# RMS norms of a decoder layer: sums and 1/sqrt on a quarter of the tokens in each of four groups of 32 columns

## The chip, the cores and the metric

One program runs on one core of one Trainium2 chip. The metric is the device time of an execution in microseconds, as the median of several runs. The core has five engines with a queue each: TensorE (PE) for matmuls, VectorE (DVE) and ScalarE (ACT) for element-wise work, GpSimd (POOL), and SyncE (SP), which here only issues transfers. PE and PEld are TensorE's matmuls and its loads of weights.

## The reference, cut to what matters

```python
def _rmsnorm(x, g):
    ...
    y = xf * lax.rsqrt(jnp.mean(xf * xf, axis=-1, keepdims=True) + EPS)
...
    h = _rmsnorm(x, norm_mix_g)
    ...
    o_dn = _rmsnorm(o_dn, dn_norm_g) * jax.nn.silu(dn_z.astype(f32).reshape(B, L, DN_HEADS, DN_DV))
    ...
    h = _rmsnorm(x, norm_ffn_g)
...
    y_prompt = _rmsnorm(xp, norm_final_g)
    y_sample = _rmsnorm(xs, norm_final_g)
```

One layer with D_MODEL 2048 runs on 576 tokens (512 of a prompt and 8 times 8 new ones). A first norm precedes the mixer, which has eight gated delta-net heads and four mLSTM heads. Each delta-net head norms its output over its 128 features (`o_dn`). After the output projection comes the second norm, then a convolutional feed-forward network (FFN), then the last norm.

## The kernel before, in words

Activations lie transposed: features on the 128 partitions, tokens along the columns. A norm therefore needs a sum over partitions. `sum_bc` (L250) makes it on PE with a 128x128 matrix of ones: its result holds each token's sum of squares on all 128 partitions, so that what follows can be multiplied onto the activations directly. It takes two matmuls of 288 tokens in plain fp32 (L256). `rsqrt_bc` (L241) then makes 1/sqrt with a table function on ACT (L244) and one Newton step in four DVE operations (L245 to L248), all 128 partitions wide and 288 or 576 columns long.

The weight matmuls are split in three of a rounded format (`three`, L194, its matmul is L198): high times high, high times low, low times high, each on two halves of 288 tokens. Six of them make a step, after which `tick` runs. A tick advances the jobs: generators, in which `yield n` means "go on n ticks later". What a job issues on PE thus falls between two groups of six L198, and PE's order is fixed by the program. The order on DVE, ACT, POOL and SP is set by a scheduler at compile time. The weights come as `raw` through SP, and ACT (L120) and DVE (L121) split them into `wh` and `wl`.

The stages, in us of the profiled execution: start until 49, the mixer's input projection with the heads as jobs beside it until about 930, the output projection from about 950 to 1152, the FFN's up projection until 2165, the down projection until 2684 with the last 16 feature blocks in `down_last`, and the last norm.

**A delta-net head** (`dn_head`, L585) is a job. It starts when its inputs are projected, every 64 ticks, and when the head before the last one has ended. It begins with transposes and small products (L608 to L663), solves for the samples through memory (L809 to L834: `ud`, `xd`, `cx` are transfers), inverts blocks of 32, 64 and 128 (`inverse`, L778, which waits for the transposes L836 and starts on PE with L843), and goes through chunks with a state S (L676 to L696). At its end it norms its output: squares on ACT, six ticks later `sum_bc`, the chain of L244 to L248, the product with `rs_o` (L710), the gate, and a transfer of the head's output.

**The second norm** is `rms_bc2` (L1075), called in `ffn` (L1118) after the matmuls of the first FFN product. The sum of squares `acc[0]` comes from L1072.

**The last norm** is in `down_last` and `final` (L1524 and what follows it). The 16 blocks of features run first on tokens 0 to 319, then on tokens 320 to 575. A block (group) is 12 matmuls L1509, the eviction L1512 on DVE, the square L1514 on ACT, in the second pass also a scaling (L1522), and on every other block an addition (L1517). Each pass spawns a job `final`: three matmuls (L1534) add up three partial sums, then ACT L1536 and DVE L1537 to L1540. The job of the first pass runs two ticks into the second pass, a tick being one group there. The second pass's job ends the program: L1551 multiplies the scaled outputs, and they are written.

Of the kernel before, what the change touches and what calls it, by code (L numbers as in the profile page):

```python
# [8 lines left out]
F32 = mybir.dt.float32  # L9
F32R = mybir.dt.float32r  # L10
AF = mybir.ActivationFunctionType
ALU = mybir.AluOpType

P = 128
D = 2048
# [53 lines left out]
class Layer:  # L69
# [180 lines left out]
    def sum_bc(self, ss):  # L250

        pss = []
        for hf in range(2):
            pr = self.psr()
            sl = slice(hf * HALF, (hf + 1) * HALF)
            self.nc.tensor.matmul(pr[:, 0:HALF], self.ones, ss[:, sl], start=True, stop=True)  # L256
            pss.append((pr[:, 0:HALF], sl))
        return pss

    def rms_bc(self, ss, out):  # L260
        self.rsqrt_bc(self.sum_bc(ss), 1.0 / D, self.eps6, EPS, out, self.r(), self.r())
# [323 lines left out]
    def dn_head(self, h, q, k, v, sz):  # L585
# [116 lines left out]


        ob, sq2 = qe, q[:, 0:NT]
        sq, rs_o, a, u = kd, vs, KQ, X
        A.activation(sq, ob, AF.Square, scale=float(P) ** -0.5)
        Pl.tensor_tensor(out=sq, in0=sq, in1=sq2, op=ALU.add)
        yield 6
        self.rsqrt_bc(self.sum_bc(sq), 1.0, self.epsh, EPS * EPS * P, rs_o, a, u)
        V.scalar_tensor_tensor(out=ob, in0=ob, scalar=self.par[:, DG:DG + 1], in1=rs_o, op0=ALU.mult, op1=ALU.mult)  # L710
        Pl.tensor_tensor(out=ob, in0=ob, in1=sz, op=ALU.mult)
        self.later(12, self.mixd[h], ob)
# [359 lines left out]
            nc.vector.tensor_tensor(out=acc[0], in0=acc[0], in1=acc[1], op=ALU.add)  # L1072


    def rms_bc2(self, ss, out):  # L1075
        nc = self.nc
        V = nc.vector
        a = self.r()
        u = self.acc[1]
        for ps, sl in self.sum_bc(ss):  # L1080
            nc.scalar.activation(out[:, sl], ps, AF.Abs_reciprocal_sqrt, bias=self.eps6, scale=1.0 / D)
            V.tensor_scalar(out=a[:, sl], in0=ps, scalar1=1.0 / D, scalar2=EPS, op0=ALU.mult, op1=ALU.add)
        V.scalar_tensor_tensor(out=u, in0=out, scalar=-0.5, in1=out, op0=ALU.mult, op1=ALU.mult)
        V.tensor_tensor(out=u, in0=u, in1=a, op=ALU.mult)
        V.scalar_tensor_tensor(out=out, in0=u, scalar=1.5, in1=out, op0=ALU.add, op1=ALU.mult)

    def conv_pads(self, f):

        rb = self.rw()
# [28 lines left out]
    def ffn(self):  # L1118
# [3 lines left out]
        fout = O["ffn_conv"].rearrange("p (s j) b w -> p s j (b w)", s=2)  # L1122
        rv = None
        self.bh, self.bl = [], []
        for j in range(NPL):
            hs = []
            for s in range(2):
                if j < NPL - 1:
                    pd = self.dense()
                else:  # L1130
                    if s == 0:
                        pds = self.dense_pair()
                        steps = self.seven_start()
                    pd = pds[s]
                if rv is None:
                    self.rms_bc2(self.acc[0], self.rstd)
                    self.close("rp", "sp")
                    b1 = self.open("b1", bufs=1, reuse_waits="tile")
                    self.rp = self.open("rb", bufs=5, reuse_waits="tile")
                    self.stg = self.open("stg", bufs=1, reuse_waits="tile")  # L1140
                    fst = self.rp.tile([P, 2, NPL, 9, 2], F32, tag="fst", name="fst0", bufs=1)
                    Pl.dma_start(out=fst.rearrange("p s j b w -> p s j (b w)"), in_=fin[:, :, 0:NPL])
                    rv = self.psum_parts(self.rstd[:, 0:HALF], self.rstd[:, HALF:NT])
                    prep = self.spawn(self.prep(0, KB1, b1), prio=False)
                rb, parts = self.conv_pads(fst[:, s, j])
                with self.urgent():
                    for o, p, r in zip(parts, self.psum_parts(pd[:, 0, 0:HALF], pd[:, 1, 0:HALF]), rv):
                        V.tensor_tensor(out=o, in0=p, in1=r, op=ALU.mult)
                hs.append((self.conv_rest(s * NF + j, rb, fst[:, s, j]), rb))
            self.hidden(j, hs[0][0], hs[1][0], hs[0][1])  # L1150
# [344 lines left out]
    def down_last(self, acts):  # L1495
# [2 lines left out]
        V, mm = nc.vector, nc.tensor.matmul  # L1498
        parts = [p for _ in range(8) for p in self.unit()]
        for sl in (slice(0, H0), slice(H0, NT)):  # L1500
            acc, xg = [self.r(), self.r()], []
            n = sl.stop - sl.start
            for m in range(KT):
                pr = self.psr()
# [16 lines left out]
                            xg.append(f.bitcast(F32)[:, 0:4 * n].rearrange("p (k t) -> p k t", k=4))  # L1521
                        nc.scalar.activation(xg[-1][:, m % 4], x, AF.Copy, scale=self.par[:, G3 + m:G3 + m + 1])  # L1522
                self.tick()
            self.spawn(self.final(sl, [*acc, sq], xg), prio=False)  # L1524
        self.finish_jobs()

    def final(self, sl, acc, xg):
        nc, O = self.nc, self.O
        V = nc.vector
        if sl.start == 0:  # L1530
            yield 2
        ps = self.psr()[:, 0:sl.stop - sl.start]
        for i, t in enumerate(acc):
            nc.tensor.matmul(ps, self.ones, t[:, sl], start=i == 0, stop=i == 2)  # L1534
        out, a, u = self.rstd[:, sl], self.r()[:, sl], acc[1][:, sl]
        nc.scalar.activation(out, ps, AF.Abs_reciprocal_sqrt, bias=self.eps6, scale=1.0 / D)  # L1536
        V.tensor_scalar(out=a, in0=ps, scalar1=1.0 / D, scalar2=EPS, op0=ALU.mult, op1=ALU.add)  # L1537
        V.scalar_tensor_tensor(out=u, in0=out, scalar=-0.5, in1=out, op0=ALU.mult, op1=ALU.mult)
        V.tensor_tensor(out=u, in0=u, in1=a, op=ALU.mult)
        V.scalar_tensor_tensor(out=out, in0=u, scalar=1.5, in1=out, op0=ALU.add, op1=ALU.mult)  # L1540
        for m in range(KT) if not xg else ():
            x = self.x2[m][:, sl]
            g = self.par[:, G3 + m:G3 + m + 1]
# [116 lines left out]
```

## Time and profile before

| | |
|---|---|
| median of 3 runs | 2697.02 us (2696.75 to 2697.04) |
| profiled execution | 2699.44 us |
| its span in the trace | 2697.7 us |
| granted TensorE clock, mean | 0.995 |
| starts of L608 in heads 0 to 3 | 115.8, 150.8, 232.2, 299.2 us |
| start of the sum in heads 0 to 3 | 220.9, 259.5, 336.1, 399.2 us |
| matmuls of L256 (two records each) | 40 records, 41.8 to 1165.7 us |

The profiled execution is one run under the profiler, and its span runs from the first to the last instruction. Lines of a timeline have the start and the length in us, the engine, the line, the operation, output and inputs, the shape, and in brackets how long the engine stood idle before and what it waited for. Records of a matmul overlap, so distances between starts tell what one costs. A plain fp32 matmul leaves two records.

### The profile page before, as it was taken

Reading aid. Unit: us, or ns where it says so; the run is one execution under the profiler, and the core shown is the slowest. Engines: PE = TensorE matmul, PEld = TensorE weight load, DVE = VectorE, ACT = ScalarE, POOL = GpSimd, SP = SyncE. Lnnn points to the kernel's source line nnn. Section 1 sums busy time; section 2 is a strip of 40 time slices with the busy share of each in tenths; the row PEclk is TensorE's granted clock in tenths of the full one; section 3 lists DMA queues with packets and bytes.
Section 4 is the critical chain, followed back from the end, with each engine's and each line's share of the span. In section 5 each row is a group of like instructions: output and inputs, shape, how many; then the busy total and the mean of one; then the engine's idle time right before and its main releaser. Section 6 shows DMA issues by size and latency. Waiting matters only on the chain.

```text
span 2697.7 us, 48872 instructions
## 1 busy us (share of the span) xinstructions
PE 2651.0 (98%) x19967; PEld 2607.0 (97%) x19967; DVE 1994.0 (74%) x3338; ACT 1080.2 (40%) x1704; POOL 333.6 (12%) x658
## 2 busy tenths in 40 slices
PE   7999999999999999998999999999999999999998
PEld 7998999999999999998999999999999999999998
DVE  7887777765544332389888888888888888888646
ACT  5334344443333322254444444444444433433324
POOL 3222322222211001101000000000000100000001
PEclk9999999999999999999999999999999999999999
DMA  5222222222333344444333333333333373342333
GB/s 195 85 77 87 90 91 91 91 88 92 114 113 104 115 135 135 135 123 150 107 111 108 108 108 108 108 108 108 108 108 109 109 256 94 106 146 71 122 97 100
DMA packets 112233, 304.02 MB, mean 113 GB/s; under 512 B 21912, under 2 KB 28184, under 8 KB 112008
## 3 DMA queue, kind: packets, MB, share of 16 engines
q1 hardware_dynamic: 107896, 291.17, 34.0%
q0 software_dynamic: 1872, 7.37, 0.8%
q8 instruction: 156, 2.56, 0.4%
q10 hardware_dynamic: 2240, 2.36, 0.3%
q14 instruction: 69, 0.57, 0.1%
HBM read 264.79 MB, written 36.06 MB: 112 GB/s over the span
## 4 chain that ended last, share of the span: by engine, by line
PE 89%; DVE 4%; DMA 1%; issue 0%; ACT 0%; POOL 0%; DVEq 0%; POOLq 0%; SPq 0%; ACTq 0%
PE pd L198 36%; PE pr L1283 31%; PE pd L1283 12%; PE pr L198 3%; PE pr L1509 1%; DVE bl L121 1%; DVE wl L121 1%; DMA r<-hid 0%; DVE r L1544 0%; PE pr L256 0%; PE pr L843 0%; PE pr L980 0%; PE pr L982 0%; PE pr L690 0%; PE pr L687 0%
## 5 line engine op out<-in xcount | busy, mean ns | idle before, releaser
L120 ACT CAST wh<-raw 128x1024 fp32r<-128x1024 f32 (+1 forms) x394 | 404.6, 1027 | 741.1 <-PE pd L198 400.2
L1283 PE MATMUL pr<-bh,wh 128*128 128x288 f32 x2120 | 626.8, 296 | 1.9 <-ACT bh L120 1.9
L1283 PE MATMUL pr<-bh,wl 128*128 128x288 f32 x2120 | 624.6, 295 | 0.5 <-DVE wl L121 0.5
L1283 PE MATMUL pr<-bl,wh 128*128 128x288 f32 x2120 | 624.3, 294 | 0.6 <-DVE bl L121 0.6
L121 DVE TENSOR_TENSOR wl<-raw,wh 128x1024 fp32r<-128x1024 f32 (+1 forms) x394 | 476.5, 1210 | 178.8 <-ACT wh L120 172.4
L198 PE MATMUL pd<-ah,wh 128*128 128x288 f32 x2496 | 560.3, 306 | 0.0
L198 PE MATMUL pd<-ah,wl 128*128 128x288 f32 x2496 | 534.5, 296 | 0.2 <-DVE wl L121 0.2
L198 PE MATMUL pd<-al,wh 128*128 128x288 f32 x2496 | 533.8, 296 | 0.0
L198 PEld LDWEIGHTS pd<-ah,wh 128*128 128x128 f32 x2496 | 401.0, 189 | 14.2 <-issue 7.7
L198 PEld LDWEIGHTS pd<-ah,wl 128*128 128x128 f32 x2496 | 401.8, 189 | 0.5 <-DVE wl L121 0.5
L198 PEld LDWEIGHTS pd<-al,wh 128*128 128x128 f32 x2496 | 401.7, 189 | 0.0
L1283 PEld LDWEIGHTS pr<-bl,wh 128*128 128x128 f32 x2120 | 400.0, 189 | 1.1 <-DVE bl L121 1.1
L1283 PEld LDWEIGHTS pr<-bh,wh 128*128 128x128 f32 x2120 | 398.4, 188 | 2.1 <-ACT bh L120 2.1
L1283 PEld LDWEIGHTS pr<-bh,wl 128*128 128x128 f32 x2120 | 398.9, 188 | 1.2 <-DVE wl L121 1.2
L120 ACT CAST wh<-s 128x1024 fp32r<-128x1024 f32 (+1 forms) x171 | 169.6, 992 | 361.2 <-DVE s L1248 142.2
L1283 PE MATMUL pd<-bh,wh 128*128 128x288 f32 x848 | 252.2, 297 | 5.6 <-ACT wh L120 5.6
L1283 PE MATMUL pd<-bh,wl 128*128 128x288 f32 x848 | 250.8, 296 | 1.7 <-DVE wl L121 1.7
L1283 PE MATMUL pd<-bl,wh 128*128 128x288 f32 x848 | 249.7, 294 | 0.0
L121 DVE TENSOR_TENSOR wl<-s,wh 128x1024 fp32r<-128x1024 f32 (+1 forms) x171 | 196.5, 1149 | 26.0 <-ACT wh L120 18.4
L1283 PEld LDWEIGHTS pd<-bh,wh 128*128 128x128 f32 x848 | 160.3, 189 | 6.1 <-ACT wh L120 6.1
L1283 PEld LDWEIGHTS pd<-bh,wl 128*128 128x128 f32 x848 | 160.6, 189 | 2.2 <-DVE wl L121 2.2
L1283 PEld LDWEIGHTS pd<-bl,wh 128*128 128x128 f32 x848 | 161.0, 190 | 0.0
(400 smaller groups left out, 3501.1 us busy)
## 6 DMA issues: line engine op xcount, KB each, us to landing
raw<-in_w_up SPq DMA_DIRECT2D x176, 512.0 KB
raw<-in_w_in SPq DMA_DIRECT2D x114, 512.0 KB
raw<-in_w_down SPq DMA_DIRECT2D x40, 512.0 KB
raw<-in_w_out SPq DMA_DIRECT2D x32, 512.0 KB
raw<-in_w_down SPq DMA_DIRECT2D x40, 384.0 KB
hid<-r SPq DMA_DIRECT2D x44, 288.0 KB
r<-hid SPq DMA_DIRECT2D x40, 288.0 KB
r<-in_xT SPq DMA_DIRECT2D x32, 288.0 KB
```

The costliest lines, as they stand in the source:

```text
L120: nc.scalar.copy(hi, src)
L121: nc.vector.tensor_tensor(out=lo, in0=src, in1=hi.bitcast(F32), op=ALU.subtract)
L198: mm(outs[hf], w, x[:, hf * HALF:(hf + 1) * HALF], start=first and i == 0, stop=last and i == 2)
L1283: mm(out, w[:, ks], x[:, sl], start=k == 0 and i == 0, stop=k == nk - 1 and i == 2)
L1509: mm(pr[:, 0:n], w[:, ks], acts[kk][:, a * NT + sl.start:a * NT + sl.stop], start=kk == 0 and i == 0, stop=kk == FB - 1 and i == 2)
```

## The change

All three norms get their sums in another form; the first norm at the start keeps `sum_bc`. The new `norm_rows` takes four matmuls with 32 columns of ones (L270 of the changed kernel), each on a quarter of the tokens and each into 32 of the 128 output partitions. Partition group j then holds the sums of quarter j, and the chain L244 to L248 runs on a quarter of the columns. The result has to come back to all partitions:

- In a delta-net head a transfer on SP writes the four rows to memory (L738), another one reads them back to 128 partitions (L740), and the product (L742, before L710) follows; four ticks lie between these steps. The head ends 12 ticks later.
- In the second and the last norm `widen` copies the four rows into a zeroed tile, two on DVE and two on ACT (L278), and `spread` multiplies it by ones (L283). The second norm becomes a job beside the first FFN product: its sum after ten ticks, its spread three ticks later, and two copies (L1155) to `rstd`.
- In the last norm's first half the spread comes two groups after the sum, with a copy to `rstd` (L1571). In its second half the products (L1583) read the spread's result directly.

```diff
+    def quarters(self, n):
+        return [(slice(32 * j, 32 * j + 32), slice(n // 4 * j, n // 4 * (j + 1))) for j in range(4)]
+
+    def norm_rows(self, srcs, n, scale, eps_col, eps, work):
+
+        q = n // 4
+        ps = self.psr()[:, 0:q]
+        for i, t in enumerate(srcs):
+            for rows, cols in self.quarters(n):
+                self.nc.tensor.matmul(ps[rows], self.ones[:, 0:32], t[:, cols], start=i == 0, stop=i == len(srcs) - 1)
+        out, a, u = (work[:, q * i:q * i + q] for i in range(3))
+        self.rsqrt_bc([(ps, slice(0, q))], scale, eps_col, eps, out, a, u)
+        return out
+
+    def widen(self, rq, wide, n):
+
+        for j, (rows, cols) in enumerate(self.quarters(n)):
+            (self.nc.scalar.copy if j % 2 else self.nc.vector.tensor_copy)(wide[32 * j:32 * j + 1, cols], rq[32 * j:32 * j + 1])
+
+    def spread(self, wide, n):
+
+        out = self.psr()[:, 0:n]
+        self.nc.tensor.matmul(out, self.ones, wide[:, 0:n], start=True, stop=True)
+        return out
...
-        sq, rs_o, a, u = kd, vs, KQ, X
+        sq, rs_o = kd, vs
...
-        self.rsqrt_bc(self.sum_bc(sq), 1.0, self.epsh, EPS * EPS * P, rs_o, a, u)
+        rq = self.norm_rows([sq], NT, 1.0, self.epsh, EPS * EPS * P, X)
+        row = self.dp.tile([1, NT], F32, tag="nrm", name=self.nm("nrm"), bufs=2)
+        yield 4
+        nc.sync.dma_start(out=row.rearrange("o (j t) -> (o j) t", j=4), in_=rq[0:P:32])
+        yield 4
+        nc.sync.dma_start(out=rs_o, in_=row.to_broadcast([P, NT]))
+        yield 4
...
+        def norm():
+            work, wide = self.r(), self.r()
+            Pl.memset(wide, 0.0)
+            yield 9
+            rq = self.norm_rows([self.acc[0]], NT, 1.0 / D, self.eps6, EPS, work)
+            self.widen(rq, wide, NT)
+            yield 3
+            for hf in range(2):
+                sl = slice(hf * HALF, (hf + 1) * HALF)
+                A.copy(self.rstd[:, sl], self.spread(wide[:, sl], HALF))
+        self.spawn(norm())
...
-                    self.rms_bc2(self.acc[0], self.rstd)
...
+        n = sl.stop - sl.start
+        rq = self.norm_rows([t[:, sl] for t in acc], n, 1.0 / D, self.eps6, EPS, work)
+        self.widen(rq, wide, n)
+        if sl.start == 0:
+            yield 2
+        out = self.spread(wide, n)
+        if not xg:
+            nc.scalar.copy(self.rstd[:, sl], out)
+            out = self.rstd[:, sl]
```

Where the instructions stand is shown at three places. The first is PE at the sum of head 0 (`r_1308` is its tile of squares, `pick` belongs to the samples' job of head 1). Before:

```order
L198 MATMUL pd_2454<-ah_113,wl_2275 128x288 x2
L256 MATMUL pr_2519<-r_1308,ones 128x288
L256 MATMUL pr_2521<-r_1308,ones 128x288
L753 MATMUL pr_2532<-r_2494,pick 32x128 x2
L198 MATMUL pd_2454<-ah_111,wh_2274 128x288 x2
```

With the change:

```order
L198 MATMUL pd_2454<-ah_113,wl_2275 128x288 x2
L270 MATMUL pr_2519<-r_1308,ones 32x144 x4
L785 MATMUL pr_2530<-r_2494,pick 32x128 x2
L198 MATMUL pd_2454<-ah_111,wh_2274 128x288 x2
L198 MATMUL pd_2454<-al_112,wh_2274 128x288 x2
```

The new sum stands at the old one's place, in front of matmuls of 32 columns. The first product of head 2 (L608, then L634) comes 54 L198 behind the sum before, nine ticks, and 126 with the change, 21 ticks.

The second place is DVE around the end of head 1's norm (`r_1638`, `r_1773` and `r_1815` are its tiles) and the solve of head 2 (`r_2710`, `cx_2890`). Before:

```order
L815 TENSOR_TENSOR r_2710<-r_2710 40x14
L817 TENSOR_TENSOR r_2710<-r_2710 40x14
L245 TENSOR_SCALAR r_1638<-pr_2998 128x288
L245 TENSOR_SCALAR r_1638<-pr_3000 128x288
L246 SCALAR_TENSOR_TENSOR r_1773<-r_1815 128x576
L121 TENSOR_TENSOR wl_2958<-raw_2955,wh_2957 128x1024
L247 TENSOR_TENSOR r_1773<-r_1773,r_1638 128x576
L549 SCALAR_TENSOR_TENSOR r_2939<-r_2939,r_2946 128x512
L834 TENSOR_TENSOR r_2709<-cx_2890,con 128x512
L834 TENSOR_TENSOR Xs_2711<-cx_2890,con 64x64
L836 STREAM_TRANSPOSE r_2710<-r_2709 128x512
```

With the change (head 2's tile is `r_2836`, its transfer `cx_3007`):

```order
L847 TENSOR_TENSOR r_2836<-r_2836 40x14
L564 TENSOR_TENSOR r_3079<-pd_2921,rstd 128x8x8
L849 TENSOR_TENSOR r_2836<-r_2836 40x14
L742 SCALAR_TENSOR_TENSOR r_1636<-r_1636,par,r_1815 128x576
L569 TENSOR_SCALAR r_3086<-r_3079,cwh 128x600
L571 SCALAR_TENSOR_TENSOR r_3086<-r_3079,cwh,r_3086 128x600 x3
L121 TENSOR_TENSOR wl_3098<-raw_3095,wh_3097 128x1024
L575 SCALAR_TENSOR_TENSOR r_3079<-r_3079,r_3086 128x512
L866 TENSOR_TENSOR r_2835<-cx_3007,con 128x512
L866 TENSOR_TENSOR Xs_2837<-cx_3007,con 64x64
L868 STREAM_TRANSPOSE r_2836<-r_2835 128x512
```

Only head 1's product L742 is left between head 2's solve and its transposes, and the convolution of later inputs (L569 to L575) stands there now; head 1's chain L245 to L248 is ahead of this piece.

The third place is ACT around the last norm's first half (`r_23776` and `r_23868` are the blocks 3 and 4 of the second pass, `r_29144` and `r_29145` are the quarters and the wide tile). With the change:

```order
L244 ACTIVATE r_29144<-pr_29470,eps_86 128x80
L1546 ACTIVATE r_29506<-r_23776 128x256
L1554 ACTIVATE xg_29434<-r_23776,par 128x256
L1546 ACTIVATE r_29524<-r_23868 128x256
L1554 ACTIVATE xg_29527<-r_23868,par 128x256
L278 COPY r_29145<-r_29144 1x80 x2
L1571 COPY rstd<-pr_29529 128x320
```

On PE the spread (`pr_29529`) stands right behind the 12 matmuls of block 4. Before, ACT had one operation for this norm at this place, L1536, ahead of the squares of block 3; now two copies and one more follow the square and the scaling of block 4 (L1546 and L1554, before L1514 and L1522).

More of the change, by code (lines that the diff above doesn't have):

```diff
@@ L1072, in square_acc2 @@
             nc.vector.tensor_tensor(out=acc[0], in0=acc[0], in1=acc[1], op=ALU.add)
[L1075 to L1085, printed above, removed]
     def conv_pads(self, f):
@@ L1500, in down_last @@
         for sl in (slice(0, H0), slice(H0, NT)):
-            acc, xg = [self.r(), self.r()], []
+            acc, xg, work, wide = [self.r(), self.r()], [], self.r(), self.r()
+            nc.gpsimd.memset(wide, 0.0)
             n = sl.stop - sl.start
@@ L1523, in down_last, with final @@
                 self.tick()
-            self.spawn(self.final(sl, [*acc, sq], xg), prio=False)
+            self.spawn(self.final(sl, [*acc, sq], xg, work, wide), prio=False)
         self.finish_jobs()
-    def final(self, sl, acc, xg):
+    def final(self, sl, acc, xg, work, wide):
         nc, O = self.nc, self.O
@@ L1531, in final @@
             yield 2
[L1532 to L1540, printed above, removed]
+        n = sl.stop - sl.start
[7 more added lines that the diff above has]
+            out = self.rstd[:, sl]
         for m in range(KT) if not xg else ():
```

## The prediction

> **What bounds the kernel now.** I read the head of the page first, then the chain of work that ended last, then what TensorE waits for in the mixer, and last the timelines at the places that the change touches.
>
> ```profile
> span 2697.7 us, 48872 instructions
> PE 2651.0 (98%) x19967; PEld 2607.0 (97%) x19967; DVE 1994.0 (74%) x3338; ACT 1080.2 (40%) x1704; POOL 333.6 (12%) x658
> PE 89%; DVE 4%; DMA 1%; issue 0%; ACT 0%; POOL 0%; DVEq 0%; POOLq 0%; SPq 0%; ACTq 0%
> ```
>
> TensorE (PE) is busy 98% of the span and holds 89% of the chain, and its order is written out by the program. So a matmul taken off PE is worth its own time, work on other engines is worth nothing until PE waits for it, and a new wait on PE costs its full length. The profiled execution took 2699.44 us, 2.42 above the median of the runs, 2697.02; the sum is made as a difference against the profiled execution and then set against the median. What PE waits for between 50 and 700 us, where the eight delta-net heads run:
>
> ```profile
> PE pr L843 <- DVE r L836: 3.1, 1, 3.1
> PE pr L657 <- DVE r L628: 1.9, 2, 1.5
> ...
> PE pr L646 <- ACT r L684: 0.6, 1, 0.6
> ...
> PE pr L687 <- ACT r L684: 0.5, 1, 0.5
> PE pr L866 <- DVE cb L799: 0.3, 1, 0.3
> ```
>
> The columns are total, count and longest, in us. The eight such lines make 8.5 us together. That is the pool from which any indirect gain must come.
>
> **Price of one sum, old and new.** The second norm's sum, and a place where 32-column matmuls already run:
>
> ```profile
> 1164.71 0.43 PE L198 MATMUL pd<-ah,wl 128*128 128x288 f32 x2
> 1164.98 1.13 PE L256 MATMUL pr<-r,ones 128*128 128x288 f32 x4
> 1165.73 0.64 PE L198 MATMUL pd<-ah,wh 128*128 128x288 f32 x2
> 1166.21 0.42 PE L198 MATMUL pd<-al,wh 128*128 128x288 f32 x2
> ...
> 179.51 0.42 PE L198 MATMUL pd<-ah,wl 128*128 128x288 f32 x2
> 179.86 0.65 PE L747 MATMUL pr<-st,kqs 128*32 128x128 f32 x16
> 180.21 0.29 PE L747 MATMUL pr<-st,kqs 128*32 128x128 f32 x4
> 180.43 0.53 PE L198 MATMUL pd<-ah,wh 128*128 128x288 f32 x2
> 180.80 0.29 PE L198 MATMUL pd<-al,wh 128*128 128x288 f32 x1
> ```
>
> Two L198 start 0.27 us apart where nothing stands between them in a pair (1164.71 to 1164.98), 0.133 each. From 1164.71 to 1166.21 lie four L198 and one old sum: 1.50 - 4x0.133 = **0.97 us**. From 179.51 to 180.80 lie four L198 and the eight matmuls of L747 (16 records, two to a matmul): 1.29 - 0.53 = 0.76 us. The last four of the 16 records, which a shorter window shows by themselves, start at 180.21, 0.35 after the first four, so groups of four records follow each other by 0.117 us, 4 groups 0.47, and 0.29 is the price of going into 32-column matmuls and out again. The new sum has four matmuls of 144 tokens, 8 records, two groups; by columns a group is 0.117x144/128 = 0.13. So 2x0.13 + 0.29 = **0.55 us**, 0.42 less per head. In head 0 the sum stands beside L753, which is in 32 columns already, so there the 0.29 goes as well. Eight heads: 8x0.42 + 0.29 = **-3.6 us**.
>
> ```profile
> L747 PEld LDWEIGHTS pr<-st,kqs x128: 106/110/110, 179.9 to 634.3; 128*32 128x32 f32 x128
> ```
>
> This row is also the test for a rule that speaks against the change. The Trainium skill ("TensorE: Matmul & The Clock Gate", the section "Part 3" on packing, under what overlaps and what doesn't) says that weight loads overlap running matmuls only where the row groups differ. Column quarters share their row groups, so by that rule eight loads of 110 ns would come on top, a sum would be 0.55 + 0.88 = 1.43 us and the heads +3.7 instead of -3.6. The trace does not agree: 16 loads would be 1.76 us, and L747 with all of its loads took 0.76.
>
> **The heads' DVE work.** The old chain on DVE is two L245 on 288 columns and L246 to L248 on 576, the new one four operations on 144.
>
> ```profile
> 228.23 0.45 DVE L245 TENSOR_SCALAR r<-pr 128x288 f32<-128x288 f32 x1
> ...
> 233.64 0.75 DVE L248 SCALAR_TENSOR_TENSOR r<-r,r 128x576 f32<-128x576 f32 x1
> 234.43 0.82 DVE L710 SCALAR_TENSOR_TENSOR r<-r,par,r 128x576 f32<-128x576 f32 x1
> ...
> 242.08 0.21 DVE L538 TENSOR_TENSOR r<-pd,rstd 128x64 f32<-128x64 f32 x1
> ```
>
> Between 0.21 at 64 columns and 0.45 at 288 an operation on 144 is about 0.29: 2x0.45 + 3x0.75 = 3.15 us fall to 1.2, 2 us of DVE per head, hidden behind PE and of use only where PE waits for DVE. The largest such place is the start of head 2. Head 0's norm (L248 and L710 at 233.6 to 235.3) runs into the inputs of head 2 there, and waits of 0.6 (L646) and 1.5 (L657) follow; 30 us later head 1's norm meets head 2's solve:
>
> ```profile
> 260.48 0.99 ACT L244 ACTIVATE r<-pr,epsh 128x288 f32<-128x288 f32 x2 [3.20 <-PE pr L256]
> ...
> 264.28 0.81 DVE L245 TENSOR_SCALAR r<-pr 128x288 f32<-128x288 f32 x2
> ...
> 269.72 0.69 DVE L834 TENSOR_TENSOR r<-cx,con 128x512 f32<-128x512 f32 x1 [1.55 <-DMA cx<-xd]
> ```
>
> The 3.1 us of L843 end in a transfer that starts after the solve, which itself ended late. With the change head 0 ends 12 ticks later, head 2 starts 12 ticks later on PE (a tick is six L198, so about 0.8 us and the head's own matmuls), the norm chain stands far ahead of head 2's first operations on DVE, and head 1's chain is out of the solve's way. These waits are 3.1 + 1.5 + 0.6 + 0.5 = 5.7 us. I take **-3.0** for them: the norm's part goes, the 1.55 us of the transfer and the waits for L684 need not. Bounds: 0 from this (the same collision 12 ticks later) and -8.5 (the whole list).
>
> The way back of the rows, to memory and out again, is new. Nearest row, a row broadcast from memory to 128 partitions:
>
> ```profile
> 217.36 0.38 SPq L592 DMA_DIRECT2D r<-rowd  x1
> ...
> 221.04 0.88 DVE L562 TENSOR_SCALAR r<-r,cols 128x128 f32<-128x128 f32 x4 [0.43 <-DMA r<-rowd]
> ```
>
> 3.7 us from issue to use. The write of the row is at least the 1.55 us that L834 stood idle for its transfer, and I take 2.5. After the sum come about 0.5 of ACT, 1.2 of DVE, 2.5 and 3.7: 8 us, against 12 ticks, at least 12x0.8 = 9.6 us. So I cost the wait at nothing, with little to spare: behind line 742 of the changed kernel in DVE's queue stand the weight split L121 and the transposes for L843, and on SP the loads of `raw` stand behind both new transfers.
>
> **The second norm.** Its sum moves to ten ticks after the start of the first FFN pair, and three ticks later come two spreading matmuls of 288 columns, as long as an old sum. PE: 0.55 + 0.97 - 0.97 = +0.55.
>
> ```profile
> 1152.18 0.42 PE L198 MATMUL pd<-ah,wh 128*128 128x288 f32 x2
> ...
> 1159.72 0.76 DVE L1072 TENSOR_TENSOR r<-r,r 128x576 f32<-128x576 f32 x1 [1.33 <-POOL r L1070]
> 1160.40 1.22 DVE L121 TENSOR_TENSOR wl<-raw,wh 128x1024 fp32r<-128x1024 f32 x1
> ```
>
> The pair's matmuls begin here at 1152.18, so ten ticks of six L198 end at 1152.2 + 60x0.133 = 1160.2; the sum of squares is there at 1159.72 + 0.76 = 1160.48: a wait of 0.3. The chain (ACT 0.35, L121 until 1161.6, four DVE operations 1.2, the copies 0.4) ends near 1163.3, and the spread comes after 18 L198, 2.4 us, at about 1163.4. Together **+1.0**, from +0.5 to +2. That rstd is ready earlier buys nothing, since PE does not wait for it.
>
> **The last norm, first half.**
>
> ```profile
> 2663.41 1.77 PE L1534 MATMUL pr<-r,ones 128*128 128x320 f32 x6
> 2664.78 0.64 PE L1509 MATMUL pr<-f,wkh 128*128 128x256 f32 x2
> 2665.26 0.28 PE L1509 MATMUL pr<-f,wkl 128*128 128x256 f32 x1
> ```
>
> With 0.12 per L1509 (256 columns), the old sum is 2665.26 - 2663.41 - 2x0.12 = 1.61, 0.27 a record. New: three sources, six groups of 0.117x80/128 = 0.073, 0.44 + 0.29 = 0.73, and a spread of 320 columns, two records, 0.54: 1.27, so -0.34. But the spread stands two groups of 12 matmuls (2.9 us) after the sum, and it waits for the copies of line 278, which on ACT stand behind the square and the scaling of group 4.
>
> ```profile
> 2683.61 0.28 PE L1509 MATMUL pr<-f,wkl 128*128 128x256 f32 x1
> ...
> 2684.21 0.42 DVE L1512 TENSOR_TENSOR r<-pr,r 128x256 f32<-128x256 f32 x1
> ...
> 2684.72 0.42 ACT L1514 ACTIVATE r<-r 128x256 f32<-128x256 f32 x1 [0.49 <-DVE r L1512]
> 2685.04 0.49 ACT L1522 ACTIVATE xg<-r,par 128x256 f32<-128x256 f32 x1
> 2685.95 0.47 ACT L1536 ACTIVATE rstd<-pr,eps 128x256 f32<-128x256 f32 x1 [0.41 <-PE pr L1534]
> ```
>
> These rows give the same steps at the end of a group: last matmul 2683.61, eviction 2684.21, square 2684.72, scaling until 2685.53, 1.92 after the last matmul's start and 1.8 after PE is free. Two copies add 0.4: PE waits **2.2 us**. First half **+1.9**, from +0.5 (the copies come first) to +3.
>
> **The last norm, second half.** It ends the span; its first half's steps on ACT stand above.
>
> ```profile
> 2686.46 0.42 DVE L1537 TENSOR_SCALAR r<-pr 128x256 f32<-128x256 f32 x1 [1.83 <-ACT rstd L1536]
> ...
> 2688.17 2.50 DVE L1551 TENSOR_TENSOR xg<-xg,rstd 128x512 f32<-128x512 f32 x4
> ```
>
> The third source is ready at 2685.14 either way (2684.72 + 0.42). Old: two records of 0.27x256/320 = 0.22 and a hand-over of 0.4, ACT at 2685.95. New: two groups of 0.06, ACT at about 2685.6, and 0.3 instead of 0.47 long; four DVE operations on 64 columns at 0.22 (the 0.21 of L538) instead of 1.71 from 2686.46 to 2688.17; then copies 0.5, spread 0.44, hand-over 0.3. Saved: 0.35 + 0.17 + 0.83 = 1.35; added 1.25, the copies and the hand-over estimated by the operation of 64 columns and by the 0.4 ahead of L1536. **-0.1**, within half a microsecond of nothing.
>
> **Sum.** -3.6 + 1.0 + 1.9 - 0.1 = -0.8 on PE and at the end, -3.0 from the waits: -3.8. 2699.44 - 3.8 = 2695.6 for a profiled execution, and 2697.02 - 3.8 = **2693.2 us** as a median.
>
> **Rivals.** (1) The waits of head 2 stay, for it still meets a norm, only later. For it: L843's wait ends in a transfer. The sum is then -0.8: 2696.2. (2) More of the list goes, and the copies overtake the square in the first half: -3.6 - 7 + 0.5 + 0.9 = -9.2, 2687.8. For it: DVE has 2 us less in each head. (3) Slower: line 742 blocks DVE. In head 3 it stands between the transposes for L843 of head 4 and the steps that follow, in heads 5 to 7 a little behind. If the rows come back 12 to 14 us after the sum instead of 8 (DVE took up head 1's sum 3.8 us after ACT, 260.48 and 264.28 above; SP holds the broadcast until the row has landed), DVE idles, and what PE lacks is 1 to 2 us a head: 6x1.5 = +9 on -0.8, 2705. It decides from about 10 us on. (4) The quarters run one after the other: eight records of 0.06 instead of two groups of 0.13 add 0.22 a head, and the sum with the waits is -2; the rows of L747 speak against it, and it would hardly show.
>
> **Chances.** Forecast 0.48, (1) 0.24, (2) 0.10, (3) 0.15, (4) 0.03. The range 2688 to 2702 takes in the first two, part of (2) and the edge of (3). A measurement here tells about 0.2%, 5.4 us, from no change: faster (below 2691.6) is (2) and a third of the forecast, 0.27; slower (above 2702.4) is most of (3), 0.12; the same 0.61.
>
> **What would show it.** Right: line 270 in groups of four records, a visit near 0.55 us; no 3.1 us wait before head 2's L843 (line 875 of the changed kernel); a wait of about 2 us on PE before the spread at 2667. Wrong: idle time of DVE ahead of line 742 put down to the transfer, followed by waits of PE in the inverse; a spread that waits in the FFN; records of line 270 that do not overlap.

## The result, and the profile after

The changed kernel takes 2716.09 us (median of 4 runs, 2715.42 to 2716.79) where the kernel before takes 2697.03: 19.06 us more, a ratio of 1.0069 with a 95% interval of 1.0056 to 1.0081. The forecast was 2693.2 us, 0.14% faster, with a range to 2702. It had the wrong sign. One execution of the kernel before, beside the experiments below, took 4272.73 us at a mean granted clock of 0.561; no ratio counts it.

The head of the page of the changed kernel, and what PE waits for between 50 and 720 us (total, times, longest, in us; L875, L672, L688 and L713 are the lines that were L843, L646, L662 and L687 before):

```profile
span 2714.4 us, 49080 instructions
PE 2657.7 (98%) x20047; PEld 2610.1 (96%) x20047; DVE 1986.1 (73%) x3335; ACT 1074.5 (40%) x1702; POOL 331.4 (12%) x661
PE 86%; DVE 5%; DMA 2%; issue 1%; ACT 1%; POOL 1%; SPq 0%; DVEq 0%; ACTq 0%; POOLq 0%
...
PE pr L875 <- issue: 6.2, 1, 6.2
PE pr L875 <- DVE r L868: 4.5, 1, 4.5
PE pr L796 <- DVE r L673: 2.0, 1, 2.0
PE pr L803 <- DVE r L673: 1.1, 1, 1.1
PE pr L688 <- DVE r L654: 1.0, 2, 0.6
PE pr L713 <- ACT r L710: 0.8, 1, 0.8
```

DVE has less to do, as planned (1986 us against 1994). The chain has lost 3% of PE to DVE and transfers: PE waits longer for them. In place of the one wait of 3.1 us at the inverse there are two, 6.2 and 4.5 us. The longer one is put down to "issue" because the profile sees no event that ends it; it ends when the transposes of head 2 are done.

Where the 19 us come from is read by setting both traces against the start of head 0, since the start-up differs from one execution to the next (its first matmul starts at 116.1 us before and at 113.6 after, in these two):

| stage, by the starts and ends in the two traces | before | after | difference |
|---|---|---|---|
| head 0's first product to the end of L1072 / L1104 | 1044.4 | 1055.7 | +11.3 |
| from there over the second norm to the first L1283 / L1314 | 69.5 | 71.4 | +1.9 |
| to the first L1509 / L1541 | 1401.0 | 1402.9 | +1.9 |
| the 384 matmuls L1509 / L1541 | 52.7 | 56.9 | +4.2 |
| tail | 14.1 | 13.8 | -0.3 |

The third row is not stable: this stage, whose code no edit here touches, took 1399.3 us in the trace of the run with the heads alone below and 1403.4 in that with head 0's tail in a job of its own. The rest is the heads, the second norm and the last norm's first half.

**The sums** behave as forecast. Timeline of PE around head 1's sum (start, length, instruction):

```profile
253.83 0.43 PE L198 MATMUL pd<-ah,wl 128*128 128x288 f32 x2
254.19 0.45 PE L270 MATMUL pr<-r,ones 128*32 128x144 f32 x8
254.57 0.53 PE L198 MATMUL pd<-ah,wh 128*128 128x288 f32 x2
254.94 0.29 PE L198 MATMUL pd<-al,wh 128*128 128x288 f32 x1
```

From 253.83 to 254.94 lie four L198 and one sum: 1.11 - 4x0.133 = 0.58 us, forecast 0.55, before 0.97. In the trace the eight records of L270 start in two groups of four, each within 0.02 us, the groups 0.15 us apart.

**Head 2** starts 12 ticks later. Before, its way to the inverse ended so:

```profile
270.46 0.70 DVE L836 STREAM_TRANSPOSE r<-r 128x512 f32<-128x512 f32 x1
...
271.21 1.16 PE L843 MATMUL pr<-r,r 128*128 128x128 f32 x8 [3.11 <-DVE r L836]
```

After, on DVE, SP and PE:

```profile
268.00 0.15 DVE L849 TENSOR_TENSOR r<-r 40x14 f32<-40x14 f32 x1
268.44 0.82 DVE L742 SCALAR_TENSOR_TENSOR r<-r,par,r 128x576 f32<-128x576 f32 x1 [0.29 <-DMA r<-nrm]
269.17 0.53 DVE L569 TENSOR_SCALAR r<-r,cwh 128x600 f32<-128x600 f32 x1
269.73 4.87 DVE L571 SCALAR_TENSOR_TENSOR r<-r,cwh,r 128x600 f32<-128x600 f32 x3
274.53 1.21 DVE L121 TENSOR_TENSOR wl<-raw,wh 128x1024 fp32r<-128x1024 f32 x1
275.67 0.68 DVE L575 SCALAR_TENSOR_TENSOR r<-r,r 128x512 f32<-128x512 f32 x1
276.27 0.68 DVE L866 TENSOR_TENSOR r<-cx,con 128x512 f32<-128x512 f32 x1
...
277.00 0.69 DVE L868 STREAM_TRANSPOSE r<-r 128x512 f32<-128x512 f32 x1
...
268.31 0.32 SPq L850 DMA_DIRECT2D xd<-r  x1
...
271.93 0.37 SPq L853 DMA_DIRECT2D cx<-xd  x1
...
271.19 0.43 PE L198 MATMUL pd<-ah,wl 128*128 128x288 f32 x2
277.80 2.05 PE L875 MATMUL pr<-r,r 128*128 128x128 f32 x8 [6.18 <-issue]
279.50 0.83 PE L198 MATMUL pd<-ah,wh 128*128 128x288 f32 x2
280.13 0.68 PE L198 MATMUL pd<-al,wh 128*128 128x288 f32 x2
```

PE is ready for the inverse at 271.6. The solve ends at 268.15, its result is sent and fetched (268.31 and 271.93), and DVE meanwhile works through a convolution of later inputs and a weight split, which stand ahead of the transposes in its order; they end at 277.7. There are 32 ticks between a head's start and its inverse, before and after. Before, PE came there 35.7 us after the head's first product (232.4 to 268.1): it had waited for 2.6 us on the way, and ten matmuls of head 1's chunks and its old sum stood among the 32 ticks. Now it comes after 31.3 us (240.3 to 271.6), with three of these matmuls and the short sum. The way over DVE and the transfers became only a little shorter, 37.4 us (240.3 to 277.7) against 38.8 (232.4 to 271.2). So the wait grew.

Only a part of it is DVE's order. Before, L834 started 1.97 us after the fetch was issued (267.75 to 269.72); by this the fetch of 271.93 would be there at about 273.9, and L866 starts at 276.27, 2.4 us later. The three L571 took 4.87 us together, where the median of this line in this trace is 0.84 each; POOL worked during most of this time (L743, L881, L857), but whether that slowed them was not tested.

And PE then runs slowly: pairs of L198 start 0.48 us apart, at 280.13 and 280.61, instead of 0.27. Stretches of the same place, with the time, busy time of PE and then of the other engines, the granted clock, the DMA share and GB/s:

```profile
275.00:277.40 2.40, 0.00 (x0) 0.00 (x0) 2.40 (x5) 0.40 (x1) 0.00 (x0) 0.75 0.28 43
277.40:280.00 2.60, 2.20 (x10) 2.23 (x11) 0.41 (x2) 0.11 (x1) 0.00 (x0) 0.50 0.72 276
280.00:282.00 2.00, 2.00 (x10) 2.00 (x9) 0.00 (x0) 0.47 (x1) 0.00 (x0) 0.50 0.00 0
282.00:284.00 2.00, 2.00 (x14) 2.00 (x13) 0.00 (x0) 0.00 (x0) 0.00 (x0) 0.74 0.04 8
284.00:286.00 2.00, 2.00 (x18) 2.00 (x17) 1.31 (x2) 0.00 (x0) 0.00 (x0) 1.00 0.00 0
```

The granted clock falls to 0.50 during the wait and comes back some 5 us after its end. L875 takes 1.0 us longer for it (2.05 us; with full clock 1.05) and 14 L198 0.107 us each: the wait of 6.2 us costs about 2.5 us more than itself.

### The profile page after: what moved, and what is told of

It is laid out like the page before. It is cut to its first block, busy times and chain, and to the rows that moved or that the text cites. A ratio compares the mean times of both kernels' runs of the same rounds, so it can differ in the third digit from the quotient of the medians.

```text
span 2714.4 us, 49080 instructions
## 1 busy us (share of the span) xinstructions
PE 2657.7 (98%) x20047; PEld 2610.1 (96%) x20047; DVE 1986.1 (73%) x3335; ACT 1074.5 (40%) x1702; POOL 331.4 (12%) x661
## 4 chain that ended last, share of the span: by engine, by line
PE 86%; DVE 5%; DMA 2%; issue 1%; ACT 1%; POOL 1%; SPq 0%; DVEq 0%; ACTq 0%; POOLq 0%
PE pd L198 33%; PE pr L1314 31%; PE pd L1314 12%; PE pr L198 3%; PE pr L1541 2%; DVE wl L121 1%; DMA r<-hid 1%; DVE r L571 1%; DVE bl L121 0%; PE pr L875 0%; DVE r L847 0%; PE pr L1012 0%; PE pr L1014 0%; PE pr L887 0%; POOL irk L647 0%
## 5 line engine op out<-in xcount | busy, mean ns | idle before, releaser
L1314 PE MATMUL pr<-bh,wh 128*128 128x288 f32 x2120 | 627.1, 296 | 2.2 <-ACT bh L120 2.2
L1314 PE MATMUL pr<-bh,wl 128*128 128x288 f32 x2120 | 624.9, 295 | 0.9 <-DVE wl L121 0.9
L1314 PE MATMUL pr<-bl,wh 128*128 128x288 f32 x2120 | 624.7, 295 | 0.7 <-DVE bl L121 0.6
L121 DVE TENSOR_TENSOR wl<-raw,wh 128x1024 fp32r<-128x1024 f32 (+1 forms) x394 | 475.8, 1208 | 165.8 <-ACT wh L120 159.1
L198 PE MATMUL pd<-ah,wh 128*128 128x288 f32 x2496 | 561.0, 306 | 0.0
L198 PE MATMUL pd<-ah,wl 128*128 128x288 f32 x2496 | 535.3, 296 | 0.3 <-DVE wl L121 0.3
L198 PE MATMUL pd<-al,wh 128*128 128x288 f32 x2496 | 534.6, 296 | 0.0
L198 PEld LDWEIGHTS pd<-ah,wh 128*128 128x128 f32 x2496 | 401.7, 190 | 15.3 <-issue 9.5
L198 PEld LDWEIGHTS pd<-ah,wl 128*128 128x128 f32 x2496 | 402.4, 189 | 0.5 <-DVE wl L121 0.5
L198 PEld LDWEIGHTS pd<-al,wh 128*128 128x128 f32 x2496 | 402.5, 189 | 0.0
L1314 PEld LDWEIGHTS pr<-bl,wh 128*128 128x128 f32 x2120 | 400.3, 189 | 1.1 <-DVE bl L121 1.1
L1314 PEld LDWEIGHTS pr<-bh,wh 128*128 128x128 f32 x2120 | 398.9, 188 | 2.4 <-ACT bh L120 2.4
L1314 PEld LDWEIGHTS pr<-bh,wl 128*128 128x128 f32 x2120 | 399.2, 188 | 1.6 <-DVE wl L121 1.6
L1314 PE MATMUL pd<-bh,wh 128*128 128x288 f32 x848 | 252.5, 298 | 5.6 <-ACT wh L120 5.6
L1314 PE MATMUL pd<-bh,wl 128*128 128x288 f32 x848 | 251.1, 296 | 1.4 <-DVE wl L121 1.4
L1314 PE MATMUL pd<-bl,wh 128*128 128x288 f32 x848 | 250.3, 295 | 0.0
L121 DVE TENSOR_TENSOR wl<-s,wh 128x1024 fp32r<-128x1024 f32 (+1 forms) x171 | 196.4, 1149 | 26.9 <-ACT wh L120 19.2
L1314 PEld LDWEIGHTS pd<-bh,wh 128*128 128x128 f32 x848 | 160.5, 189 | 6.1 <-ACT wh L120 6.1
L1314 PEld LDWEIGHTS pd<-bh,wl 128*128 128x128 f32 x848 | 161.1, 190 | 2.0 <-DVE wl L121 2.0
L1314 PEld LDWEIGHTS pd<-bl,wh 128*128 128x128 f32 x848 | 161.3, 190 | 0.0
```

The source lines that it names most:

```text
L121: nc.vector.tensor_tensor(out=lo, in0=src, in1=hi.bitcast(F32), op=ALU.subtract)
L198: mm(outs[hf], w, x[:, hf * HALF:(hf + 1) * HALF], start=first and i == 0, stop=last and i == 2)
L1314: mm(out, w[:, ks], x[:, sl], start=k == 0 and i == 0, stop=k == nk - 1 and i == 2)
```

## The experiments

Two theories of the heads' loss. **One:** the harm is in the end of a head, 12 ticks later, which shifts the start of the next head but one against the other work. **Two:** it is in the rows' way through memory, for which DVE stops ahead of the product (it does: 5.2 us in four of the eight heads, in the view of DVE's waits). The kernel before, run beside each set, took 2697.08 us (19 runs), 2698.13 and 2698.46 us (31 runs each) in the median; single runs of it lay from 2694 to 2703, so a difference of a few us is read from the ratio and its interval.

### One part alone

Each of the first three has one of the change's three parts and the rest of the kernel before. For the heads:

```diff
+        rq = self.norm_rows([sq], NT, 1.0, self.epsh, EPS * EPS * P, X)
+        row = self.dp.tile([1, NT], F32, tag="nrm", name=self.nm("nrm"), bufs=2)
+        yield 4
...
+        yield 4
...
+        yield 4
```

> Only the delta-net heads have the new norm (quarters, rows through memory, 12 ticks more); second and last norm as before. Both theories on the heads expect what the two traces show up to the end of the mixer, +11.2 us: 2708 us (2706 to 2710). If the heads' part only looked so because of the other edits, it is within 3 us of 2697.

Measured: 2708.97 us, ratio 1.0044 (1.0029 to 1.0059), +11.9. The trace has the waits of 6.3 and 4.5 us at the inverses of heads 2 and 4.

For the second norm, `norm` as a job of `ffn` in place of `rms_bc2`:

```diff
+            rq = self.norm_rows([self.acc[0]], NT, 1.0 / D, self.eps6, EPS, work)
+            self.widen(rq, wide, NT)
+            yield 3
...
-                    self.rms_bc2(self.acc[0], self.rstd)
```

> Only the second norm is changed. By the traces of before and after +2.0 us in the first FFN product (0.6 of matmuls, 1.4 of waits): 2699.0 us (2698 to 2700). If the 2 us that the changed kernel loses later in the FFN and the down projection also hang on this norm (another order on VectorE), 2701.

Measured: 2700.05 us, 1.0010 (1.0000 to 1.0019), +3.0. In its profiled execution PE fell to half clock after a wait of 2.5 us in head 2, where this kernel is as before, so that part of the 3 us may be chance. In its trace the stage of the second norm is 2.0 us longer than before (71.45 against 69.45).

For the last norm:

```diff
+        rq = self.norm_rows([t[:, sl] for t in acc], n, 1.0 / D, self.eps6, EPS, work)
+        self.widen(rq, wide, n)
+        if sl.start == 0:
+            yield 2
+        out = self.spread(wide, n)
```

> Only the last norm is changed. By the traces +4.2 us in its first half (a wait of 2.7 us ahead of the spread and then TensorE at half clock for some 3 us) and -0.3 at the end: 2701 us (2700 to 2702). My forecast of the wait alone, without the clock, gives +1.8: 2698.8.

Measured: 2701.78 us, 1.0017 (1.0008 to 1.0027), +4.7. The wait ahead of the first spread is 2.4 us, with the clock at 0.50 for three microseconds after it. The three parts add up: 11.9 + 3.0 + 4.7 = 19.6, against 19.1.

### The delay without the new norm

```diff
         self.rsqrt_bc(self.sum_bc(sq), 1.0, self.epsh, EPS * EPS * P, rs_o, a, u)
+        yield 12
         V.scalar_tensor_tensor(out=ob, in0=ob, scalar=self.par[:, DG:DG + 1], in1=rs_o, op0=ALU.mult, op1=ALU.mult)
```

> The kernel before, with twelve more ticks between each head's norm chain and its product, so that each head ends 12 ticks later; no quarters, no rows through memory. Theory one (the later end shifts the start of head 2 against the other heads' work, and TensorE then waits for the solve and its transposes): the mixer loses the waits and the half clock but gains no shorter sums, +11.2 + 3.6 = +14.8, 2712 us (2706 to 2715), with a wait over 4 us at the inverse of head 2. Theory two (VectorE waits for the rows from memory, and what is queued behind it comes late): no change, 2697 us (2695 to 2699).

Measured: 2715.89 us, 1.0071 (1.0056 to 1.0086), +18.8. That is theory one, and more than it asked for. What PE waits for in the mixer:

```profile
PE pr L844 <- issue: 11.1, 1, 11.1
PE pr L844 <- DVE r L837: 4.8, 1, 4.8
PE pr L765 <- DVE r L647: 2.0, 1, 2.0
```

The same two inverses, with 11.1 us at head 2. Here head 1's long chain (L247 and L248 on 576 columns) still stands between the steps of head 2's solve, which ends at 276.8 instead of 268.15. So the new norm does help at that place, by 4.9 us of wait. L247, L248 and the product L711 take 2.3 us of the solve there, and the convolution (L543, L545) stands inside it too; what share each has was not measured. The delay costs more than this help.

### The rows without the delay

What follows the sum becomes a job of its own, so that the head counts as ended at the sum:

```diff
+        def tail():
+            yield 4
+            nc.sync.dma_start(out=row.rearrange("o (j t) -> (o j) t", j=4), in_=rq[0:P:32])
+            yield 4
+            nc.sync.dma_start(out=rs_o, in_=row.to_broadcast([P, NT]))
+            yield 4
...
+        self.spawn(tail())
```

> Only the heads have the new norm, as in the first run, but what follows the sum (rows out, rows back, product) is a job of its own, so that a head counts as ended at the sum, where it ended before, and the next head but one starts at the old tick. Theory one (the later end does the harm): the short sums are left, 2697 - 3.6 and up to 2 us of waits at head 2 less, 2692.5 us (2690 to 2695). Theory two (VectorE stops ahead of the product until the rows are back): the rows take the same way, so the loss stays, 2705 to 2709.

Measured: 2695.43 us, 0.9991 (0.9981 to 1.0001), -2.7. The loss is gone, the gain is smaller than expected and not clear of nothing. PE's waits in the mixer are 9.6 us in its trace; four of them, 2.8 us together, stand at L800 in later heads and wait for ACT (L723). In the next one only head 0 is treated so:

```diff
+        if h == 0:
+            self.spawn(tail())
+        else:
+            yield from tail()
```

> As the run before, but only head 0 has its tail in a job of its own; heads 1 to 7 end 12 ticks later. Theory one in its narrow form (the only start that hangs on an earlier head's end is that of head 2, since later heads start when their inputs are projected): like the run before, 2692.5 us (2690 to 2695), with no wait of over 2 us at the inverse. If every head's later end does harm by itself, 2700 or more, with the wait of 4.5 us at head 4 still there.

Measured: 2691.74 us, 0.9978 (0.9968 to 0.9987), -6.4. It is the only kernel here that is clearly faster than the kernel before. The waits of PE in its mixer are 5.9 us, without those for ACT L723; a tail in a job of its own seems to pay only where a start would move. The largest two and the one at the inverse:

```profile
PE pr L673 <- ACT r L711: 1.9, 1, 1.9
PE pr L810 <- DVE r L674: 1.1, 1, 1.1
...
PE pr L882 <- DVE r L875: 0.5, 1, 0.5
```

DVE still stops for the rows there, 4.8 us in four heads:

```profile
DVE r L745 <- DMA r<-nrm: 4.8, 4, 2.1
```

So theory two falls: the stops are there, and after three of them (405, 473 and 542 us) PE has no wait until 560. The narrow form of theory one stands: one late end, of head 0, makes the whole loss of the heads.

### Which start costs what

Where a head's first product stands on PE, in ticks (L198 counted in program order, divided by six):

| kernel | h0 | h1 | h2 | h3 | h4 | h5 | h6 | h7 |
|---|---|---|---|---|---|---|---|---|
| before | 117 | 154 | 223 | 282 | 346 | 410 | 474 | 538 |
| changed | 117 | 154 | 235 | 282 | 348 | 410 | 474 | 538 |

Head 2 starts when head 0 has ended. Heads from 3 on start when their inputs are there, every 64 ticks, but head 2's end came 24 ticks later and pushed head 4 by two. The next two kernels move one of these starts each: heads 1 to 7 with tails of their own (head 2 at 235, head 4 at 346), and the kernel with only head 0's tail in its own job, with 12 more ticks at head 2's end (head 2 at 223, head 4 at 348).

```diff
+        if h > 0:
+            self.spawn(tail())
+        else:
+            yield from tail()
```

> Only the heads have the new norm; heads 1 to 7 have their tails in own jobs, head 0 ends 12 ticks late. On TensorE head 2 then starts at tick 235 as in the changed kernel (223 before), head 4 at 346 as before (348 in the changed kernel). If the harm sits in the two starts that moved: the wait of 6 us and the half clock at head 2 are there, the wait at head 4 is not, so the heads' +12 of the first run less 7 to 8: 2701 us (2699 to 2703). If one late start is enough for all of the later waits, 2707 or more.

Measured: 2699.07 us, 1.0003 (0.9993 to 1.0012), +0.6. The wait at head 2 is 6.1 us, that at head 4 0.4. Against the run with only head 0's tail in its own job this is 7.0 us more, but there the tails of heads 1 to 7 differ too. The run that differs in head 0's tail alone is the one with every tail in its own job, -2.7: the late head 2 costs 3.3 us, with intervals that overlap. PE's waits for ACT L723 (2.8 us) are in both.

```diff
             yield from tail()
+            if h == 2:
+                yield 12
```

> As the run with only head 0's tail in its own job, but head 2 holds its successor up for 12 ticks more, so that head 4 starts at tick 348, two later, and every other head where it started before. If two ticks decide at head 4: a wait of 4.5 us at its inverse with half clock behind it, 7 to 8 us more than without, 2699 us (2697 to 2702). If head 4's wait in the changed kernel came from head 2's late work and not from its own two ticks, 2692 us (2690 to 2694).

Measured: 2704.89 us, 1.0021 (1.0011 to 1.0031), +6.4, which is 13 us more than without these two ticks. In the traces 10.4 us of it lie between head 0's start and the second norm's sum of squares, and 1.0 at the end of the kernel, where another order on DVE makes the last sum wait for 1.5 us instead of 0.5. From here to the run with the heads alone (+11.9) head 2's start moves as well: 5.5 us more. The wait at head 4's inverse is 4.4 us with half clock behind it, and a new wait of 2.0 us follows in head 5 (L805). Why two ticks decide is seen on DVE. Head 4 with its start at 346 (only head 0's tail in a job of its own): its solve begins at L848 and ends at L856, and the convolution of later inputs (L570, L572) runs inside it:

```profile
374.53 0.23 DVE L838 TENSOR_TENSOR cb<-r 128x64 f32<-128x64 f32 x1
...
375.70 0.45 DVE L563 TENSOR_TENSOR r<-pd,rstd 128x288 f32<-128x288 f32 x1
...
378.35 1.13 DVE L848 TENSOR_SCALAR r<-r 40x256 f32<-40x256 f32 x1 [0.38 <-DMA r<-ud]
...
381.17 0.51 DVE L570 TENSOR_SCALAR r<-r,cwh 128x600 f32<-128x600 f32 x1
...
390.44 0.17 DVE L856 TENSOR_TENSOR r<-r 40x14 f32<-40x14 f32 x1
```

With its start at 348 (the same steps are L840, L563, L850 and L858):

```profile
378.11 0.44 DVE L563 TENSOR_TENSOR r<-pd,rstd 128x288 f32<-128x288 f32 x1
...
380.50 1.29 DVE L840 TENSOR_TENSOR cb<-r 128x64 f32<-128x64 f32 x1
...
384.48 1.72 DVE L572 SCALAR_TENSOR_TENSOR r<-r,cwh,r 128x600 f32<-128x600 f32 x2
...
388.27 0.28 DVE L850 TENSOR_SCALAR r<-r 40x256 f32<-40x256 f32 x1
...
399.29 0.84 DVE L572 SCALAR_TENSOR_TENSOR r<-r,cwh,r 128x600 f32<-128x600 f32 x1
...
401.99 0.15 DVE L858 TENSOR_TENSOR r<-r 40x14 f32<-40x14 f32 x1
```

Now the inputs' rows (L563) come ahead of the step L840 that feeds the solve's first transfer, the whole convolution stands ahead of the solve, and the next convolution, 16 ticks on, falls into it. From the head's first product to the solve's end it takes 33.1 us (369.05 to 402.14) instead of 26.2 (364.42 to 390.61), with the same 32 ticks on PE. The order on DVE is what the scheduler makes of the new start; whether another order at the same start would save the time was not tried.

A start 11 ticks late instead of two:

```diff
             yield from tail()
+            if h == 2:
+                yield 21
```

> As the run before it, with 21 ticks instead of 12: head 4 starts at tick 357, 11 later. If a later start is bad in proportion, over 2702. If it depends on where the start falls against the other heads' work, anything between 2690 and 2705, and the wait at head 4's inverse in the trace tells which.

Measured: 2703.91 us, 1.0020 (1.0010 to 1.0029), +5.5, with a wait of 5.5 us at head 4. So the loss is not in proportion to the delay; two ticks are as bad as eleven.

### The two spreads

The last norm alone, with the first spread five groups after the sum:

```diff
-            yield 2
+            yield 5
         out = self.spread(wide, n)
```

> Only the last norm is changed, and the spread of its first half comes five groups after the sum instead of two. The copies stand at the same place on ScalarE, so TensorE no longer waits there and stays at full clock: -0.3 - 0.3, 2696.5 us (2695.5 to 2697.5), 4 to 5 us less than with two groups. If what costs is the spread itself or VectorE's later outputs, it stays near 2701.

Measured: 2699.42 us, 1.0005 (0.9996 to 1.0014), +1.3 where -0.6 was expected and two groups gave +4.7. In the trace the wait of the first half is gone, and the 384 matmuls take 52.35 us (before 52.68, with two groups 56.58). From the end of the last of them to the end of the last operation that is no transfer it takes 10.0 us instead of 9.2, since products of the first half now come later on DVE and the last sum waits 0.8 us for an addition there.

The second norm alone, with its spread six ticks after the sum:

```diff
-            yield 3
+            yield 6
             for hf in range(2):
```

> Only the second norm is changed, and its spread comes six ticks after the sum instead of three. The wait ahead of the spread, 1.2 us by the trace of the changed kernel, is gone, the 0.2 ahead of the sum stays, and 0.6 of matmuls are added: 2698 us (2697 to 2699), 1.2 us less than with three ticks.

Measured: 2698.02 us, 0.9999 (0.9990 to 1.0009), -0.4, and +3.0 with three ticks (in another set). The wait ahead of the spread is gone in the trace, and the second norm's stage takes 70.28 us, 1.2 less than with three ticks.

All three norms, with every head's tail in its own job and both later spreads:

> All three norms changed, with every head's tail in its own job, the second norm's spread six ticks after the sum instead of three and the last norm's first spread five groups after it. By theory one: heads -3.6 to -5, second norm +0.6, last norm -0.6, so 2692.5 us (2690 to 2695).

Measured: 2699.93 us, 1.0003 (0.9994 to 1.0013). That is 7 us more than expected and 4.5 us more than the heads' part of it alone. The traces give 0.8 us of these 4.5 to the second norm's stage, 0.5 to the stage of the heads and 0.5 to the last norm; the rest was not found. Beside the heads' part the other two norms bring nothing in this form.

## Why the prediction was wrong, point by point

- **The sums of the heads: right.** 0.58 us a visit against 0.55. The quarters run beside each other, in groups of four records as I had named it for a sign. Rival (4) was priced too low: records of L256 with 288 columns start 0.24 us apart, so eight of 144 one after another would take about 0.97 us, not 8x0.06. The rule on weight loads in the Trainium skill ("TensorE: Matmul & The Clock Gate", Part 3), by which a visit would take 1.43 us, does not hold here.
- **The waits of head 2, taken as -3.0: this step failed, and its sign.** In place of waits of 5.7 us there are 6.6 (6.2 and 0.4), and half clock for another 2.5: +3.4. I wrote that "the norm's part goes" when head 2 starts 12 ticks later. The norm's chain did go out of the way, and against the delayed old norm the wait at the inverse is 6.2 instead of 11.1 us. But I treated the later start as harmless and asked only whether the same collision came back, so that 0 was my upper bound. I also added up the four waits as if each could go by itself: the 2.6 us ahead of the inverse did fall to 0.4, and PE only stood there sooner. What bounds the way to the inverse is 32 ticks of PE against a way over DVE and the transfers that takes about 37 us there; a start at another tick changes what else falls into each. The rows of the order that I showed had the convolution and a split (L569 to L575, L121) in front of the transposes, and I read them as an improvement.
- **Head 4: not in the sum at all.** Its start moved by two ticks, from 346 to 348, which the order of PE shows when the ticks are counted for every head; I counted for head 2 alone. By themselves these two ticks cost 13 us in the medians, more than the late head 2, which costs 3.3 or 5.5 us by the two pairs of runs above. With both starts kept the heads bring -6.4, near the -3.6 - 3.0 of the forecast, but that is partly luck: the wait at head 2's inverse falls from 3.1 to 0.5 us, and another one (L673, before L646) rises from 0.6 to 1.9.
- **The clock: not in the sum.** After the long waits PE ran at half speed, which cost about 2.5 us at head 2 and 2.8 us at head 4 in the changed kernel. PE's waits between 50 and 720 us are 16.8 us against 8.5; with 5.3 of half clock and -3.1 of shorter sums that makes +10.5 of the 11.3 in the heads' stage.
- **The rival on the slower side** had the wrong mechanism. My 8 us for the rows' way were too short: in the four heads of the changed kernel where DVE waits for the rows, they come 10.2 to 14.3 us after the sum, beyond the 10 us from which this was to decide. DVE stops for the rows as it said, and PE does not feel it.
- **The second norm: +1.0 forecast, +2.0 in the trace.** The chain was mis-sized. I let the table load of ACT run ahead of the sum; here it starts behind it, the spread waits, and the price is 1.2 us:

```profile
1169.94 1.28 ACT L244 ACT_TABLE_LOAD   x1 [1.51 <-PE pr L270]
...
1173.31 1.24 PE L283 MATMUL pr<-r,ones 128*128 128x288 f32 x4 [0.90 <-ACT r L278]
```

- **The last norm's first half: the wait right, its price short.** 2.2 us forecast; the changed kernel's trace has 2.7, for the reason given, copies behind the square and the scaling of block 4:

```profile
2681.27 0.42 ACT L1546 ACTIVATE r<-r 128x256 f32<-128x256 f32 x1 [1.23 <-DVE r L248]
2681.60 0.49 ACT L1554 ACTIVATE xg<-r,par 128x256 f32<-128x256 f32 x1
2682.10 0.52 ACT L278 COPY r<-r 1x80 f32<-1x80 f32 x2
...
2682.67 1.43 PE L283 MATMUL pr<-r,ones 128*128 128x320 f32 x2 [2.72 <-ACT r L278]
2683.44 1.09 PE L1541 MATMUL pr<-f,wkh 128*128 128x256 f32 x2
```

  The half clock behind it makes +4.2 of the forecast +1.9.
- **The last norm's second half: right,** -0.3 against -0.1.

## What to carry to other kernels

In a kernel whose TensorE order is written out and whose other engines work in order behind it, a delay that costs nothing at its own place can move the start of a later stage, and two ticks of such a shift cost more here (13 us) than eight shortened sums can bring (8x(0.97 - 0.58) = 3.1 us). When an edit adds steps to a job, count on TensorE's order where every job that waits for its end will start, and give the added steps a job of their own where a start would move, and only there. A wait of several microseconds is to be priced with the half clock that follows it.

## What the runs showed of the hardware that I had not expected

The granted clock fell to 0.50 after every wait of PE of 4.4 us and more in the heads, and after some shorter ones: after 2.7 and 2.4 us ahead of the first spread (changed kernel and the last norm alone), after 2.5 us at head 2 (the second norm alone) and after 1.9 us at L673 (the run with head 0's tail in its own job and the two with head 4 late, each with half clock for 3.4 us). It did not fall after 1.9 us at L673 with every tail in its own job, nor after 2.7 us at head 2 with the second norm's later spread, nor after 3.1 us at head 2 in the kernel before, nor after 3.5 us at the first norm (L256) with every tail in its own job. So here a wait between 1.9 and 3.5 us can cost its length or some 2 us more; what decides it was not found. The Trainium skill ("TensorE: Matmul & The Clock Gate", the section "Why this matters for your kernels") warns of idle gaps over about 3 us; the gaps of 1.9 to 2.7 us that were followed by half clock lie below that.
